# The second score product over 128 rows: the keys' low part as a tile per head

## The chip, the cores and the metric

One core of a Trainium2 chip runs the whole kernel in one launch. The metric is the time of one execution on the device in microseconds (us), as the median of several runs. A core has a tensor engine (PE, which multiplies a stationary tile, held in its array, with a moving one that streams through), VectorE (DVE), ScalarE (ACT), GpSimd (POOL), and SyncE (SP), whose queue issues almost all DMA transfers here. Each engine works through its own instructions in their order and waits for others by semaphores.

## The reference

Two layers of a decoder trunk on 512 tokens of 1024 features. Each layer has a SwiGLU feed-forward part (FFN), a token mixing and a second FFN, each behind an RMSNorm with a shift and scale from a condition vector. The mixing has 16 heads of 64 features in three groups:

```
scale = 64 ** -0.5
A (4 heads): softmax(q k' * scale, causal) v            # block-sparse; at 512 tokens every causal key is selected
B (4 heads): softmax over the 128 best causal keys of each query, ranked by an indexer:
             I[t, s] = sum_j w[t, j] * relu(q_idx[t, j] . k_idx[s])      # 8 indexer heads of 64
C (8 heads): stick-breaking: sigmoid(z) * prod over later keys of (1 - sigmoid(z)),  z = q k' * scale, s < t
o = headRMS(concat(A, B, C)) * out_g;   x = x + g2 * (o @ w_out)
```

q and k of groups A and B are normed per head and partly rotated; those of the indexer are rotated. All is float32.

## The kernel before, in words

Activations lie with features on partitions and tokens along the free axis. PE takes float32r operands; a float32 value v is carried as two of them, H = float32r(v) and L = float32r(v - H). A large product (`mm3`, lines 308 to 310) is three products added in PSUM: H.H, H.L and L.H. Weights come from HBM in pieces of 128 x 1024: SP loads a piece (`raw`, line 268, three buffers), ACT takes its H (`whi`, line 270), VectorE its L (`wlo`, line 280).

Scores contract over the 64 features of a head, half of the 128 partitions. The two heads of a pair lie on the two halves. To fill the rows, the kernel stacks parts. The q of head e is one tile whose own half (64 rows) holds H and whose other half holds L. The k of head e is one tile with H on both halves. One product over 128 rows then gives Hq.Hk + Lq.Hk. The missing Hq.Lk is a second product into the same PSUM area. It contracts over the 64 rows of the head's own half, and one tile holds the L of both heads' keys, each on its own half. So score products come in pairs, the first 128 rows deep, the second 64 rows deep (line 612).

The tiles are made so. ACT writes H of both heads (line 577) and VectorE L (line 578), each over 128 partitions. Then SP copies halves from partition to partition by DMA (`move`, line 603): three copies for a q pair, three for a k pair. All these tiles come from one pool of 12 buffers of 128 x 512, `qk`. A new tile waits until an older one is released by its last reader. The indexer's k is written with its two halves equal from the start and needs no copy.

The scores of a pair of heads come in three units. Unit 0 holds query tiles 0 and 1 of both heads: eight score products, four of 256 and four of 128 columns. Units 1 and 2 hold query tiles 2 and 3 of one head each. In group C they have keys on partitions and eight products (six of 256, two of 128 columns). In groups A and B they have queries on partitions and four products (two of 512, two of 384). The indexer has eight heads, each with four such products for query tiles 2 and 3, and for query tile 1 eight products of 256 columns for every four heads. Per layer this makes 208 score products. After the scores come the weights on ACT and VectorE, products with a triangular matrix (group C, line 705) or transpositions (A and B, line 769), then the outputs (line 656): eight products per unit over 128 rows.

The work of a layer's mixing is cut into steps, and a list, `PLAN`, names the order in which they are issued. The build's scheduler then moves instructions within it. Projections, which are long runs of `mm3`, stand between the steps of the attention, as does the top-k of group B, long runs of VectorE work (lines 853 and 854).

Of the kernel before, what the change touches and what calls it, by code (L numbers as in the profile page):

```python
"""Two layers of a conditioned hybrid decoder trunk on one core.

Activations are feature-major ([feature, token]) on chip, so that every weight is used in its own
layout as the stationary operand.  A float32 operand of a large product is carried as two float32r
parts, H = float32r(v) and L = float32r(v - H), and a product is H.H + H.L + L.H in float32 PSUM.

With 512 tokens and blocks of 256 there is at most one past block per query, and the block
top-k always selects it: group A attends to every causal key.  Group B's queries t < 128 have at
most 128 causal keys, all of which its top-128 holds; later tiles rank their keys on chip.
"""  # L10
# [16 lines left out]
P = 128  # L27
# [9 lines left out]
HD = 64  # L37
# [10 lines left out]
# Score tiles of a pair of heads come in three units, each two PSUM banks wide: query tiles 0 and 1  # L48
# of both heads (a bank each), then query tiles 2 and 3 of each head.  A block is (head, index, column in PSUM,
# column in SBUF, width).  # L50
#   with keys on partitions: index is the key chunk, and its columns are the unit's queries from
#   that chunk on; with queries on partitions: index is the query tile, and its columns its keys.
# [15 lines left out]
# Small constants: name, shape in a partition, needed by the first norm or later.  # L68
# [12 lines left out]
def head_chunks(l, f):  # L81
    """d_ff chunks that run side by side at the start of an FFN, while its input is still being made."""
    return list(range(4 if (l, f) == (0, 0) else 2))
# [41 lines left out]
# The order in which the steps of the mixing are issued.  A name that comes again is the next step of  # L125
# the same work: u = a unit of a pair's attention (scores and weights, their transposition or sums,
# outputs), n = norm of a pair's heads, c = q and k of a pair of group C, a and b = q and k of groups
# A and B, i = indexer scores, t = top-k of a query tile, v = values, h = split of a pair's output,
# o = output projection of group C.  w loads a weight piece ahead of its use.
# [53 lines left out]
class Net:  # L183
# [24 lines left out]
    def load(self, names, early):  # L208
        """One tile of small constants: a view per name."""
        shapes = [(n, s) for n, s, e in SMALL if e == early]  # L210
        t = self.cp.tile([P, sum(int(np.prod(s)) for _, s in shapes)], F32, name=names)
        self.nc.sync.dma_start(t, self.io[names])
        o, out = 0, []
        for _, s in shapes:
            w = int(np.prod(s))
            v = t[:, o:o + w]
            if len(s) > 1:
                names_ = "abc"[:len(s)]
                v = v.rearrange("p (%s) -> p %s" % (" ".join(names_), " ".join(names_)),
                                **{c: int(d) for c, d in zip(names_, s)})  # L220
            out.append(v)
            o += w
        return out

    def setup(self):
        """What the first norm needs."""
        nc = self.nc
        self.tc.keep_in_program_order(nc.scalar.preload_act_table_set("silu_and_others"))
        for m in range(0, KC, 2):
            nc.sync.dma_start(self.xs[:, m:m + 2, :], self.io["x"][:, m:m + 2, :])  # L230
        self.open_ada()
        self.first_w = [self.load_ada(0, 1, 0, 6)]
        self.normg, self.bada = self.load("early", True)
        self.first_w.append(self.load_ada(0, 0, 0, 6))
        self.ident = self.t(self.fp, "ident", [P, P])
        nc.sync.dma_start(self.ident, self.io["ident"])
        ones = self.cp.tile([P, 4], F32, name="ones")
        nc.gpsimd.memset(ones, 1.0)
        nc.gpsimd.memset(ones[HD:, 2:3], 0.0)
        nc.gpsimd.memset(ones[:HD, 3:4], 0.0)  # L240
        self.ones2, self.bones = ones[:, 0:2], ones[:, 2:4]
        self.mod = {}
# [19 lines left out]
    def fetch(self):  # L262
        """Loads a weight piece and takes its H."""
# [30 lines left out]
    def later(self, us, fn):  # L294
        """Has fn emitted once products of about us more microseconds have been."""
        self.delayed.append([us, fn])
# [16 lines left out]
    def rsqrt(self, ss, shape, inv, r=None, wide=None, pin=False):  # L313
        """With r: of ss * r * r * inv, and times r.  wide: where to write each, repeated."""
# [53 lines left out]
    def ada_first(self):  # L368
        """The shift and scale of the first norm, feature chunk by feature chunk."""
# [8 lines left out]
    def ada_all(self, items):  # L378
        """Modulation vectors, a half of one at a time."""
# [22 lines left out]
    def norm_rms(self, cs, pin=False):  # L402
        """1 / rms of the tokens of cs, a token tile per column."""
# [8 lines left out]
    def norm_wide(self, y, cs):  # L412
        """The same over all partitions."""
# [39 lines left out]
    def ffn_head(self, l, f, halves, prepare=lambda k: None):  # L453
        """First products of the FFN, chunk by chunk of its input."""
# [17 lines left out]
    def ffn(self, l, f, filler, head):  # L472
        """Generator: yields (m, tokens) for each finished part of the output."""
# [68 lines left out]
    def proj_tok(self, l, grp, tiles, evac):  # L542
        """Token-major projection, two steps per token tile: evac(t, psum)."""
# [27 lines left out]
    # Scores contract over 64 features: H.H and L.H go together, as a head's q with H on its own half  # L571
    # of the partitions and L on the other, and its k with H on both.
# [7 lines left out]
    def put_q(self, out, ps, scale=1.0, lo=0):  # L580
        """Features of a pair of heads, from token lo on, in two steps: adds a tile per head."""
# [9 lines left out]
    def put_k(self, out, ps, scale=1.0):  # L591
        """Adds a tile of H per head, and one of L, in two steps."""
        a, b, l = self.new_qk(3)
        self.split_feat(ps, scale, a, l)
        out.append((a, b, l))
        yield
        self.move(b[HD:], a[HD:])
        self.move(b[:HD], a[HD:])
        self.move(a[HD:], a[:HD])
        yield  # L600
# [4 lines left out]
    def scores(self, out, q, k, e, qs, ks, keys_out, start, stop):  # L605
        """Products of a head's q and k: of the columns qs and ks, with keys on partitions or queries."""
        own = slice(64 * e, 64 * e + 64)
        parts = [(q[e][:, qs], k[e][:, ks]), (q[e][own, qs], k[2][own, ks])]
# [6 lines left out]
    def do_rope(self, x, heads, tiles, table):  # L615
        """x: [P, len(tiles), heads, HD] view, rotated in place."""
# [12 lines left out]
    def to_feat(self, src, tiles, put):  # L629
        """src(t): token-major [P, 128] -> put(features by tokens), a step and those of put."""  # L630
# [6 lines left out]
    # Values of a pair of heads: token tile, head, H or L, feature.  A head's H and L are stationary  # L637
    # together, and their products with the weights are added when they leave PSUM.
# [3 lines left out]
    def put_v(self, v, t, ps):  # L642
        """ps: [P, 128] of one pair of heads."""
# [4 lines left out]
    def unit_out(self, pair, u, z, att):  # L648
        """Outputs of a unit, in its score tile, in two steps."""
# [18 lines left out]
    def finish_pair(self, l, pair, cs=slice(0, S)):  # L668
        """RMSNorm of both heads of a pair, in five steps."""
# [26 lines left out]
    def stick(self, pair, q, k, u):  # L696
        """Stick-breaking attention of a unit, keys on partitions, in seven steps."""
# [40 lines left out]
    def soft(self, pair, q, k, u, bias):  # L738
        """Softmax attention of a unit, queries on partitions, in seven steps.  The weights stay without
        their sums' division, which the norm of the heads makes up for.  # L740
        bias(t): [P, 128 * (t + 1)] added to the scores of query tile t."""
# [33 lines left out]
    def index_k(self, l):  # L775
# [30 lines left out]
        def put(ps):  # L806
# [3 lines left out]
            self.qk["ki"] = hi, hi, lo  # L810
# [15 lines left out]
    def index_heads(self, heads):  # L826
        """Adds four indexer heads to the scores, in ten steps."""
# [19 lines left out]
    def topk(self, t):  # L847
        """The top-128 keys of a query tile (lowest index first among equals) as an additive bias."""
# [11 lines left out]
    def gained_rope(self, l, gi):  # L860
        """The rotation's tables times a gain, and the gain of the other features on partitions."""
# [9 lines left out]
    def qk_ab(self, l, name, grp, gi):  # L871
        """Normed, rotated q and k of a pair of heads of group A or B, feature-major."""
# [46 lines left out]
    def finish_half(self, l, cs):  # L919
        """The last pair's norm and split for a token half."""  # L920
        yield from self.finish_pair(l, 3, cs)
        self.split_o(3, cs)
        yield

    def steps(self, l):
        """The mixing's work by name, each a generator of its steps."""
# [62 lines left out]
    def out_first(self, l, m):  # L989
        """Output projection of group C, in two steps."""  # L990
# [7 lines left out]
    def out_last(self, l):  # L998
        """Output projection of groups A and B, and the start of the next norm."""
# [20 lines left out]
    def ffn_norm(self, out, l, i):  # L1020
        """Adds up the next norm as the FFN's output comes."""
# [127 lines left out]
```

## Time and profile before

| | |
|---|---|
| median of 3 runs | 2210.2 us (2207.52 to 2212.14) |
| span of the profiled execution (first to last instruction) | 2206.9 us |
| mean granted PE clock | 0.991 |
| score products | 416, first at 431.4 us, last at 1794.2 us |

The profiled execution's own time is its span, 2206.9 us; the runs of the table were not profiled. In the profile each engine has busy times; PE's products are pipelined, so the times of single products overlap, and PEld is the loading of the stationary tile, which has an instruction of its own. A group row reads: line, engine, operation, output<-inputs, shape, number | busy us, mean ns of one | idle time before them and what ended it. `64*128` before the shape means 64 rows and 128 columns of the array. A row of stretches reads: stretch, its length, then busy us and instructions of each engine, the granted clock as a share of full speed, the DMA engines' busy share, and GB/s. A row of waits reads: who waited for whom, us in total, times, longest. A row of DMA issues ends with the us from issue to landing. The chain is the work that ended last, followed back from the end, without overlaps.

### The profile page before, as it was taken

The numbers are of one execution on the slowest core, as the hardware profiler recorded it, in microseconds if no ns is written. First come the engines' busy times: TensorE is split into PE (matmuls) and PEld (weight loads), VectorE is DVE, ScalarE is ACT, GpSimd is POOL, SyncE is SP. The second block draws the span as 40 slices with busy tenths as digits, with TensorE's granted clock in tenths as the row PEclk, the third lists the DMA queues.
The fourth block names the chain that finished last, engine by engine and source line by source line (L and its number), as shares of the span: only waits on it lengthen the run. The fifth ranks groups of instructions, "written<-read, shape, count | busy, mean of one in ns | idle before, by whom it ended". The sixth has DMA issues, their size and how long they took to land.

```text
span 2206.9 us, 28693 instructions
## 1 busy us (share of the span) xinstructions
PE 2171.1 (98%) x11280; PEld 1833.1 (83%) x11280; DVE 1308.5 (59%) x2607; ACT 832.6 (38%) x1295; POOL 3.5 (0%) x12
## 2 busy tenths in 40 slices
PE   6999999999999999999999999999999999999999
PEld 5888888878988988888898888887788888888888
DVE  8663744679979777375374333364799787333332
ACT  3422222456655432132242222234565644222220
POOL 0000000000000000000000000000000000000000
PEclk9999999999999999999999999998999999999999
DMA  7873842431222378385243333324222222333331
GB/s 292 272 267 97 288 140 82 111 80 50 76 70 80 120 249 283 99 267 191 86 132 115 96 96 97 96 73 115 58 71 65 75 72 87 96 96 96 97 98 63
DMA packets 82310, 275.45 MB, mean 125 GB/s; under 512 B 9984, under 2 KB 12544, under 8 KB 82176
## 3 DMA queue, kind: packets, MB, share of 16 engines
q1 hardware_dynamic: 80736, 271.53, 39.6%
q8 instruction: 88, 1.44, 0.3%
q10 hardware_dynamic: 1440, 2.10, 0.3%
q14 instruction: 46, 0.38, 0.1%
HBM read 256.55 MB, written 2.10 MB: 117 GB/s over the span
## 4 chain that ended last, share of the span: by engine, by line
PE 92%; DVE 5%; DMA 2%; ACT 1%; issue 1%; DVEq 0%; ACTq 0%
PE z L308 23%; PE z L310 23%; PE z L309 23%; PE z L612 6%; PE b L308 4%; PE b L310 4%; PE b L309 4%; PE z L656 2%; PE z L705 1%; DVE wlo L280 1%; DMA raw<-in_w_dram 1%; PE z L769 1%; DMA qk<-qk 1%; DVE att L568 1%; PE b L679 1%; PE b L633 1%
## 5 line engine op out<-in xcount | busy, mean ns | idle before, releaser
L280 DVE TENSOR_TENSOR wlo<-raw,whi 128x1024 fp32r<-128x1024 f32 (+1 forms) x338 | 412.2, 1220 | 542.1 <-ACT whi L270 540.1
L270 ACT CAST whi<-raw 128x1024 fp32r<-128x1024 f32 (+1 forms) x338 | 354.6, 1050 | 876.0 <-PE z L309 789.1
L308 PE MATMUL z<-hh,whi 128*128 128x512 f32 (+1 forms) x1616 | 597.2, 370 | 6.7 <-DVE xs L986 3.9
L309 PE MATMUL z<-hl,whi 128*128 128x512 f32 (+1 forms) x1616 | 597.2, 370 | 0.5
L310 PE MATMUL z<-hh,wlo 128*128 128x512 f32 (+1 forms) x1616 | 596.2, 369 | 1.3 <-DVE wlo L280 1.3
L308 PEld LDWEIGHTS z<-hh,whi 128*128 128x128 f32 x1616 | 306.0, 190 | 58.6 <-DVE xs L986 4.3
L310 PEld LDWEIGHTS z<-hh,wlo 128*128 128x128 f32 x1616 | 306.1, 190 | 52.7 <-DVE wlo L280 1.8
L309 PEld LDWEIGHTS z<-hl,whi 128*128 128x128 f32 x1616 | 306.4, 190 | 52.1 <-DVE hl L430 1.3
L308 PE MATMUL z<-gh,whi 128*128 128x512 f32 (+1 forms) x792 | 293.5, 371 | 0.0
L309 PE MATMUL z<-gl,whi 128*128 128x512 f32 (+1 forms) x792 | 292.8, 370 | 0.0
L310 PE MATMUL z<-gh,wlo 128*128 128x512 f32 (+1 forms) x792 | 289.1, 370 | 0.0
L349 DVE CUSTOM_DVE_ANT_0 adaw<-adaw,silc 128x1024 f32<-128x1024 f32 x144 | 170.9, 1221 | 30.1 <-DMA adaw<-in_w_ada_dram 30.1
L308 PEld LDWEIGHTS z<-gh,whi 128*128 128x128 f32 x792 | 149.0, 188 | 29.6
L310 PEld LDWEIGHTS z<-gh,wlo 128*128 128x128 f32 x792 | 149.1, 188 | 27.6
L309 PEld LDWEIGHTS z<-gl,whi 128*128 128x128 f32 x792 | 149.1, 188 | 26.5
L308 PE MATMUL b<-whi,hh 128*128 128x256 f32 x544 | 158.1, 291 | 0.0
L309 PE MATMUL b<-wlo,hh 128*128 128x256 f32 x544 | 156.1, 287 | 0.0
L310 PE MATMUL b<-whi,hl 128*128 128x256 f32 x544 | 156.0, 287 | 0.0
L612 PE MATMUL z<-qk,qk 64*128 64x256 f32 (+7 forms) x416 | 138.3, 392 | 1.5 <-DMA qk<-qk 1.5
L612 PEld LDWEIGHTS z<-qk,qk 128*128 128x128 f32 (+1 forms) x416 | 78.5, 189 | 56.9 <-issue 26.6
L506 DVE SCALAR_TENSOR_TENSOR xs<-z,mod,xs 128x512 f32<-128x512 f32 (+1 forms) x72 | 49.7, 691 | 124.5 <-PE z L310 124.4
L308 PEld LDWEIGHTS b<-whi,hh 128*128 128x128 f32 x544 | 105.7, 194 | 1.2 <-issue 0.6
(144 smaller groups left out, 2348.3 us busy)
## 6 DMA issues: line engine op xcount, KB each, us to landing
raw<-in_w_dram SPq DMA_DIRECT2D x332, 512.0 KB, 3.6
adaw<-in_w_ada_dram SPq DMA_DIRECT2D x144, 512.0 KB, 4.7
qk<-qk SPq DMA_DIRECT2D x96, 128.0 KB, 2.2
qk<-qk SPq DMA_DIRECT2D x24, 96.0 KB, 3.0
xs<-in_x_dram SPq DMA_DIRECT2D x4, 512.0 KB, 5.7
raw<-in_w_dram SPq DMA_DIRECT2D x4, 492.0 KB, 3.4
silc<-in_c_dram SPq DMA_DIRECT2D x3, 512.0 KB, 5.1
out_dram<-xs ACTq DMA_DIRECT2D x6, 256.0 KB, 2.0
```

The source lines that it names most:

```text
L270: nc.scalar.copy(hi[:, :n], raw[:, :n])
L280: self.nc.vector.tensor_sub(lo[:, :n], raw[:, :n], hi.bitcast(F32)[:, :n])
L308: mm(out, l[0], r[0], start=start, stop=False, **kw)
L309: mm(out, l[0], r[1], start=False, stop=False, **kw)
L310: mm(out, l[1], r[0], start=False, stop=stop, **kw)
L349: r = self.nc.vector.tensor_tensor_reduce(w, w, self.silc, 1.0, 0.0, op0=ALU.mult, op1=ALU.add, accum_out=m[:, j:j + 1])
L506: nc.vector.scalar_tensor_tensor(self.x[m][:, cs], ps[:, cs], gate[:, m:m + 1], self.x[m][:, cs], op0=ALU.mult, op1=ALU.add)
L568: nc.vector.tensor_sub(unit_sbuf(lo, u), src, unit_sbuf(hi.bitcast(F32), u))
L612: self.nc.tensor.matmul(out, a, b, start=start and i == 0, stop=stop and i == 1, skip_group_check=True)
L633: self.nc.tensor.transpose(ps[:, t * P:(t + 1) * P], src(t), self.ident)
L656: nc.tensor.matmul(outs[e][:, HT - w:], lhs, a[:, o:o + w], start=i + j == 0, stop=c == KEY_UNITS[u][-1][1] and j == 1, skip_group_check=True)
L679: nc.tensor.matmul(ss[:, i, :], sq[:, t * P:(t + 1) * P], self.bones, start=True, stop=True)
```

## The change

The L of the keys gets the same treatment as the H: one tile per head with L on both halves of the partitions. The second score product then takes the whole q tile and the whole L tile of its head, 128 rows. It adds Hq.Lk + Lq.Lk, so the sum now holds the product of the two low parts as well, which the kernel before left out.

```diff
     def put_k(self, out, ps, scale=1.0):
-        a, b, l = self.new_qk(3)
+        a, b, l, m = self.new_qk(4)
         self.split_feat(ps, scale, a, l)
-        out.append((a, b, l))
+        out.append((a, b, l, m))
         yield
-        self.move(b[HD:], a[HD:])
-        self.move(b[:HD], a[HD:])
-        self.move(a[HD:], a[:HD])
+        for own, other in ((a, b), (l, m)):
+            self.move(other[HD:], own[HD:])
+            self.move(other[:HD], own[HD:])
+            self.move(own[HD:], own[:HD])
         yield

     def scores(self, out, q, k, e, qs, ks, keys_out, start, stop):
-        own = slice(64 * e, 64 * e + 64)
-        parts = [(q[e][:, qs], k[e][:, ks]), (q[e][own, qs], k[2][own, ks])]
+        parts = [(q[e][:, qs], k[i + e][:, ks]) for i in (0, 2)]
         for i, (a, b) in enumerate(parts):
             if keys_out:
                 a, b = b, a
             self.nc.tensor.matmul(out, a, b, start=start and i == 0, stop=stop and i == 1,
                                   skip_group_check=True)
...
-            self.qk["ki"] = hi, hi, lo
+            self.qk["ki"] = hi, hi, lo, lo
```

A k pair takes four tiles from the pool of 12 and six copies; there are eight k pairs in a layer, so 48 copies more in all. Comments were removed too, which shifts line numbers by one or two.

The change also moves instructions. SP, in the mixing of layer 0, at q and k of the second pair of group B (the last in the layer); `qk_1000` to `qk_1002` are its q tiles before, `qk_1025` and `qk_1026` its H tiles of k. Before:

```order
L268 DMA raw_1104_6451<-in_w_dram 128x1024
L603 DMA qk_1001_5953<-qk_1000_5952 64x512
L603 DMA qk_1001_5953<-qk_1002_5954 64x512
L603 DMA qk_1000_5952<-qk_1002_5954 64x512
L268 DMA raw_1107_6457<-in_w_dram 128x1024
L603 DMA qk_1026_6067<-qk_1025_6066 64x512 x2
L603 DMA qk_1025_6066<-qk_1025_6066 64x512
L268 DMA raw_1110_6463<-in_w_dram 128x1024
```

And now, with `qk_1007` to `qk_1009` for q, `qk_1032` and `qk_1033` for H of k, `qk_1034` and `qk_1035` for its L:

```order
L268 DMA raw_1112_6483<-in_w_dram 128x1024
L605 DMA qk_1008_5981<-qk_1007_5980 64x512
L605 DMA qk_1008_5981<-qk_1009_5982 64x512
L605 DMA qk_1007_5980<-qk_1009_5982 64x512
L268 DMA raw_1115_6489<-in_w_dram 128x1024
L605 DMA qk_1033_6095<-qk_1032_6094 64x512 x2
L605 DMA qk_1035_6097<-qk_1034_6096 64x512 x2
L605 DMA qk_1032_6094<-qk_1032_6094 64x512
L268 DMA raw_1118_6495<-in_w_dram 128x1024
L605 DMA qk_1034_6096<-qk_1034_6096 64x512
L268 DMA raw_1133_6632<-in_w_dram 128x1024
```

The copies of L go between those of H, and a weight load that followed the third copy now has three more copies around it.

PE, where that pair's unit 0 takes its scores, before:

```order
L690 MATMUL b_1038_6133<-rmat_513,of_965_5785 128x128 x3
L612 MATMUL z_1028_6078<-qk_1025_6066,qk_1000_5952 128x256
L612 MATMUL z_1028_6078<-qk_1027_6068,qk_1000_5952 128x256
L612 MATMUL z_1028_6078<-qk_1026_6067,qk_1001_5953 128x256
L612 MATMUL z_1028_6078<-qk_1027_6068,qk_1001_5953 128x256
L612 MATMUL z_1028_6078<-qk_1025_6066,qk_1000_5952 128x128
```

And now:

```order
L613 MATMUL z_1036_6110<-qk_1032_6094,qk_1007_5980 128x256
L770 MATMUL z_1041_6140<-rmat_513,tf_1023_6029 128x128 x7
L691 MATMUL b_1046_6165<-rmat_513,of_972_5813 128x128
L308 MATMUL b_1069_6270<-hh_970_5809,whi_1015_6006 128x512
L309 MATMUL b_1069_6270<-hl_971_5810,whi_1015_6006 128x512
L613 MATMUL z_1054_6206<-qk_1033_6095,qk_1008_5981 128x512
L613 MATMUL z_1054_6206<-qk_1035_6097,qk_1008_5981 128x512
L613 MATMUL z_1054_6206<-qk_1033_6095,qk_1008_5981 128x384
L613 MATMUL z_1054_6206<-qk_1035_6097,qk_1008_5981 128x384
L613 MATMUL z_1036_6110<-qk_1034_6096,qk_1007_5980 128x256
L613 MATMUL z_1036_6110<-qk_1033_6095,qk_1008_5981 128x256
L613 MATMUL z_1036_6110<-qk_1035_6097,qk_1008_5981 128x256
```

The second product reads `qk_1034` for head 0 and `qk_1035` for head 1, where before both read `qk_1027`. The scheduler put other work of PE between the first product and the first that needs the L tiles. Over the whole program the order on PE differs only in such places, and the splits of q and k on ACT stand where they stood.

## The prediction

> **What bounds the kernel now.** I read the page's busy shares first, then the chain that ended last, then the waits of PE in the mixing of layer 0, then which lines fill that chain.
>
> ```profile
> span 2206.9 us, 28693 instructions
> PE 2171.1 (98%) x11280; PEld 1833.1 (83%) x11280; DVE 1308.5 (59%) x2607; ACT 832.6 (38%) x1295; POOL 3.5 (0%) x12
> ...
> PE 92%; DVE 5%; DMA 2%; ACT 1%; issue 1%; DVEq 0%; ACTq 0%
> PE z L308 23%; PE z L310 23%; PE z L309 23%; PE z L612 6%; PE b L308 4%; PE b L310 4%; PE b L309 4%; PE z L656 2%; PE z L705 1%; DVE wlo L280 1%; DMA raw<-in_w_dram 1%; PE z L769 1%; DMA qk<-qk 1%; DVE att L568 1%; PE b L679 1%; PE b L633 1%
> ```
>
> The tensor engine (PE) is busy for 98% of the span and makes 92% of the chain. The score products, L612, are 6% of the chain: some 132 us, and all of it lies in the two mixings, nowhere in the FFNs. The longest wait of PE between 420 and 860 us is this one:
>
> ```profile
> PE z L308 <- DVE xs L986: 1.9, 1, 1.9
> ```
>
> So in the mixing PE hardly waits for anybody, and what makes its own instructions shorter is worth something until another engine falls behind. The question is how long a score product takes, and who is next.
>
> **What a score product costs.** Two rows of the groups by shape, and the row of all of them:
>
> ```profile
> L612 PE MATMUL z<-qk,qk 64*128 64x256 f32 (+7 forms) x416 | 138.3, 392 | 1.5 <-DMA qk<-qk 1.5
> ...
> L612 PE MATMUL z<-qk,qk 64*128 64x384 f32 x32 | 14.6, 455 | 0.0
> L612 PE MATMUL z<-qk,qk 128*128 128x384 f32 x32 | 14.5, 452 | 0.0
> ```
>
> These durations overlap one another, so they do not show the price. Starts do. From the timeline of PE:
>
> ```profile
> 433.23 0.28 PE L308 MATMUL b<-whi,hh 128*128 128x256 f32 x1
> 433.35 1.22 PE L612 MATMUL z<-qk,qk 128*128 128x256 f32 x4
> 434.49 0.39 PE L309 MATMUL b<-wlo,hh 128*128 128x256 f32 x1
> ...
> 469.69 0.39 PE L308 MATMUL b<-hh,whi 128*128 128x512 f32 x1
> 469.92 3.16 PE L612 MATMUL z<-qk,qk 128*128 128x512 f32 x8
> ```
>
> An ordinary product of 256 columns is followed by the next start after 0.12 us (433.23 to 433.35), one of 512 after 0.23 us (469.69 to 469.92). In both places the product that follows is the first of a score group, a 128-row one, and it starts on time. But four score products of 256 columns take 1.14 us (433.35 to 434.49), 0.285 each. They alternate between 128 and 64 rows, so each one stands beside a product of another row count. The chain of waits gives the same for each kind of group (start, us on the chain):
>
> ```profile
> 433.51 1.05 PE z L612 x4
> ...
> 470.08 3.00 PE z L612 x8
> ...
> 502.79 0.23 PE b L310
> ...
> 503.71 2.07 PE z L612 x8
> ...
> 573.09 2.19 PE z L612 x8
> ...
> 614.98 0.90 PE z L656 x8
> ```
>
> The outputs of a unit, L656, are the twin of its scores: eight products, the same column counts, a new stationary tile each, always 128 rows. They take 0.90 us, the scores 2.07 (unit 0) or 2.19 (units 1 and 2 of group C). I read the difference as a price of every change of the row count, about 0.16 us, which the change removes by making all scores 128 rows deep.
>
> One rule of the Trainium skill speaks against this reading: the page "TensorE: Matmul & The Clock Gate", Part 3, The mechanism, says that a weight load overlaps running matmuls only when it goes to another row group. By it, making both kinds 128 rows deep would gain nothing. This trace contradicts it: products of 128 rows, each with its own load, start 0.12 us apart. The page "TensorEngine Tiling (Array Packing)", Key Properties, says that changing the tiling mode drains the array; that fits, but no run here shows a drain as such. No number below needs either page.
>
> **The change, part by part.**
>
> *Score products.* Per layer, at the chain's prices: 8 units of index 0: 2.07 - 0.90 = 1.17 each, 9.4 us. 8 units 1 and 2 of group C: 2.19 - 0.90 = 1.29, 10.3 us. 16 groups of 512+512+384+384 columns (8 softmax units, 8 indexer heads): 3.00 / 2 = 1.50 now; at 0.23 and, between 0.12 and 0.23, 0.175 for 384 columns, 0.81 after; 0.69 each, 11.0 us. Two indexer units of eight 256-column products: 2 x 1.05 = 2.10 now, 0.96 after, 2.3 us in all. Together 33 us a layer, 66 in both. From the other side, the whole 138.3 us busy against 192 x 0.12 + 64 x 0.23 + 64 x 0.175 + 96 x 0.09 = 58 us leaves 80; 0.09 for 128 columns is the rest of L656's 0.90 after six of 0.12. I take 72, which is 0.52 of L612's busy time, of which the larger bound counts overlapping ends.
>
> *Clock.* Around the densest score groups the granted clock drops:
>
> ```profile
> 1518.00:1548.00 30.00, 28.89 (x110) 0.77 0.31 84
> ```
>
> 0.23 x 30 = 6.9 us are lost there alone. If the gate follows how dense the array's work is, part of it comes back. From nothing to 7 us; I take 4, since a good half of it lies on L612 itself and is in the 72 already.
>
> *What VectorE leaves.* This decides how much of the 72 is kept. Stretches of the two mixings, all engines (PE, PEld, DVE, ACT, POOL), then L612 alone in the same stretches:
>
> ```profile
> 420.00:480.00 60.00, 59.02 (x273) 42.80 (x273) 32.96 (x57) 29.02 (x40) 0.00 (x0) 0.97 0.36 93
> 480.00:620.00 140.00, 139.58 (x896) 123.16 (x895) 129.19 (x329) 89.30 (x144) 0.00 (x0) 0.99 0.26 69
> 620.00:740.00 120.00, 119.79 (x825) 105.98 (x825) 96.36 (x300) 65.03 (x151) 0.00 (x0) 1.00 0.27 83
> 1509.00:1569.00 60.00, 58.26 (x240) 41.53 (x239) 28.84 (x48) 24.86 (x35) 0.00 (x0) 0.89 0.34 87
> 1569.00:1709.00 140.00, 139.53 (x873) 121.91 (x874) 127.88 (x318) 87.70 (x135) 0.00 (x0) 0.98 0.25 66
> 1709.00:1829.00 120.00, 119.74 (x829) 106.40 (x829) 95.25 (x306) 65.67 (x155) 0.00 (x0) 1.00 0.24 68
> ```
>
> ```profile
> 420.00:480.00 60.00, 24.96 (x72) 13.41 (x72) 0.97 0.36 93
> 480.00:620.00 140.00, 25.01 (x84) 15.53 (x84) 0.99 0.26 69
> 620.00:740.00 120.00, 18.01 (x52) 9.63 (x52) 1.00 0.27 83
> 1509.00:1569.00 60.00, 24.67 (x67) 13.22 (x67) 0.89 0.34 87
> 1569.00:1709.00 140.00, 27.74 (x90) 17.04 (x90) 0.98 0.25 66
> 1709.00:1829.00 120.00, 17.96 (x52) 9.62 (x52) 1.00 0.24 68
> ```
>
> First stretch (indexer scores, first pair of C): PE saves 0.52 x 24.96 = 13.0 us and VectorE is busy for 33 of 60, so all of it counts; 12.8 in layer 1. Second stretch: PE could save 13.0 (14.4), but VectorE already works 129.2 (127.9) of 140, so no more than 10.8 (12.1) can be had, and its handing over to ACT and back is in those gaps. I take 4.5 in each layer, between 0 and 11. Third stretch: 9.4 (9.3) on PE against 96 of 120 on VectorE; I take 8. Sum 25.5 + 25.3 = 51.
>
> *More copies.* Each of the 16 key tiles now needs six SBUF copies instead of three: 48 more.
>
> ```profile
> qk<-qk SPq DMA_DIRECT2D x96, 128.0 KB, 2.2
> ...
> L603 SPq DMA_DIRECT2D qk<-qk x120: 461/462/785, 421.3 to 1781.9; - x120
> ...
> 681.34 5.51 SPq L603 DMA_DIRECT2D qk<-qk  x3
> ...
> 689.33 2.32 PE L612 MATMUL z<-qk,qk 128*128 128x256 f32 x8
> ```
>
> The third copy of a tile overwrites what the first two read, so it waits for a landing (2.2 us). The two chains run one inside the other: the new one adds three issues of 0.46 us, 1.4 us, to SP for each key, and at most 1.4 + 2.2 = 3.6 us if its landing is paid apart. Behind them in SP's queue stand weight loads. Mostly the scores come 10 us and more after the copies. At the last pair of group B they do not: the three copies end at 686.85, the last lands 2.2 us later, about 689.0, and the scores start at 689.33. There 1.4 us is late; likewise the weight loads behind it. I charge 3 us in all, between 0 and 16 x 3.6 = 58.
>
> *Tiles and instructions on ACT and VectorE.* The fourth tile of a key is written by copies alone: ACT and VectorE get no instruction more, and the products' count stays 416.
>
> Sum: 51 + 4 - 3 = 52 us. The profiled execution's span is 2206.9 us, 3.3 below the median of 2210.2, so I take the difference off the median: 2158 us.
>
> **Rivals.** *VectorE lets PE have it all*: its order carries the slack of the thin stretches over. For it: it is idle for 41% of the span. Against: its 92% in the second stretch. 66 to 87 us less: 2123 to 2144, say 2134. *VectorE takes nearly all*: behind the first stretch the chains PE, ACT, VectorE, PE get no shorter. For it: PE and VectorE are both over 90% there. Only the first stretches count, 26 us less 3: 2187. *The row count is not what costs*: L612 is slow for a reason that both forms share, such as its weight load in the same rows. For it: 452 against 455 ns above. Against: the first product of each group starts on time, and L656. Then nothing is gained and 3 us are lost: 2213, within the noise. *The pool of 12 tiles runs dry, slower than before*: a key now holds four tiles to the end of its pair's scores instead of three, so copies wait for older scores, and weight loads wait behind them on SP.
>
> ```profile
> SPq L603 <- PE z L612: 8.4, 2, 4.2
> ```
>
> This has happened twice, at 4.2 us each. If it comes with every key and each also pays the 3.6 us, a key costs 7.8 us; ten of the 16 reaching PE undo the 72, fourteen cost 109 and give 2210 + 37 = 2247. Against it: in the order of the changed kernel the splits of q and k on ACT stand where they stood, and PE has other products between.
>
> **How the numbers follow.** The forecast, 2158 (own range 2144 to 2175), has 0.62; all to PE 0.14; VectorE takes nearly all 0.14; no gain 0.05; pool dry 0.05. Differences under 0.2%, 4.4 us, count as none. The first three are faster: 0.90; same 0.05, slower 0.05. The range holds the forecast, most of the full gain and the nearer half of the third: 2128 to 2188.
>
> **What would show it.** Right: no 64-row form of the score line; a softmax unit's four scores at about 0.8 us on the chain and a unit's eight at 0.9; L612's share of the chain from 6% to under 3%; new waits of PE for VectorE or ACT in the second stretch and VectorE's share there above 95%; the granted clock in the first stretch of layer 1 above 0.89. Wrong: eight scores still near 2 us (then the row count was not the cause), or PE waiting for copies or weights by more than some us a layer.

## The result, and the profile after

| | before | changed kernel |
|---|---|---|
| median, first comparison | 2211.17 us (2207.52 to 2212.47) | 2145.63 us (2145.13 to 2149.47) |
| ratio, 95% interval | | 0.9714 (0.9700 to 0.9727) |
| median, a second comparison | 2206.94 us | 2146.83 us, 0.9720 (0.9702 to 0.9737) |
| span of the profiled execution | 2206.9 us | 2147.7 us |
| mean granted PE clock | 0.991 | 0.996 |

The changed kernel is 60 to 66 us faster, 2.8 to 2.9%. 52 us were forecast. The page of its profile, the parts that answer to those shown of before:

```profile
span 2147.7 us, 28762 instructions
PE 2094.9 (98%) x11280; PEld 1806.0 (84%) x11280; DVE 1305.2 (61%) x2607; ACT 831.2 (39%) x1295; POOL 2.9 (0%) x12
...
PE 82%; DVE 12%; ACT 2%; DMA 2%; issue 1%; SPq 0%; ACTq 0%; DVEq 0%
PE z L308 23%; PE z L310 23%; PE z L309 23%; PE b L308 3%; PE b L310 3%; PE b L309 3%; DVE att L568 2%; DVE sc L855 2%; DVE wlo L280 2%; DVE m L854 1%; PE z L613 1%; DMA qk<-qk 1%; PE z L657 1%; PE z L706 1%; DVE tf L718 1%
```

The score products, now line 613, went from 6% of the chain to 1%. VectorE went from 5% to 12%: chain pieces in the mixing now run through its top-k and its splits. The chain of the changed kernel (start, us on the chain):

```profile
532.66 0.90 PE z L613 x8
...
608.98 0.88 PE z L657 x8
...
616.40 0.81 PE z L613 x4
...
626.44 0.88 PE z L613 x8
```

Eight scores now take what eight outputs (L657) take, 0.88 to 0.90 us instead of 2.07 to 2.19. Four scores of a softmax unit take 0.81 instead of 1.50. No 64-row form of the line is left. The timeline says the same of four products of 256 columns, which took 1.14 us:

```profile
433.30 0.64 PE L613 MATMUL z<-qk,qk 128*128 128x256 f32 x4
433.77 0.28 PE L309 MATMUL b<-wlo,hh 128*128 128x256 f32 x1
```

That is 0.47 us from start to start, 0.12 each. Added up over all 416 from the trace's records, the time from the start of a score product to the start of PE's next product fell from 134.2 us to 68.5. At 0.12, 0.23, 0.175 and 0.09 us for the four widths it would be 58.

Stretches of the mixings in the changed kernel (columns as before). They lie near the work of the earlier ones, but do not hold the same: the second of layer 0 has 806 of PE's products, not 896.

```profile
420.00:470.00 50.00, 46.59 (x274) 40.61 (x274) 30.84 (x54) 27.23 (x38) 0.00 (x0) 0.97 0.46 118
470.00:590.00 120.00, 115.53 (x806) 106.71 (x805) 118.01 (x295) 83.33 (x129) 0.00 (x0) 0.99 0.32 85
590.00:707.00 117.00, 114.18 (x846) 106.90 (x845) 99.67 (x312) 66.50 (x158) 0.00 (x0) 1.00 0.36 102
1484.00:1530.00 46.00, 42.99 (x259) 37.19 (x258) 30.09 (x52) 25.36 (x36) 0.00 (x0) 1.00 0.45 119
1530.00:1660.00 130.00, 125.51 (x888) 116.67 (x887) 127.88 (x324) 89.35 (x140) 0.00 (x0) 0.99 0.33 87
```

In the second stretch VectorE is at 98% of the time (118.0 of 120, 127.9 of 130), and PE, at 99.7% before, at 96%. How long the same work takes is read from the starts of the products that have the same number in PE's order (about 2% of the products stand elsewhere in that order, so this holds to about 1 us). Lengths in us:

| stretch before | before | changed, first and second profile | saved | forecast |
|---|---|---|---|---|
| 420 to 480 | 60 | 49.9, 48.0 | 10 to 12 | 13.0 |
| 480 to 620 | 140 | 130.8, 130.0 | 9 to 10 | 4.5 |
| 620 to 740 | 120 | 114.9, 115.0 | 5 | 8 |
| 1509 to 1569 | 60 | 43.9, 43.0 | 16 to 17 | 12.8 |
| 1569 to 1709 | 140 | 128.4, 127.6 | 12 | 4.5 |
| 1709 to 1829 | 120 | 114.5, 114.4 | 5 to 6 | 8 |

PE now waits where it hardly waited before (1.5 us for the copies, 0.2 for `att`, nothing listed for `v`):

```profile
PE z L613 <- DMA qk<-qk: 5.5, 5, 1.9
PE z L657 <- DVE att L568: 4.7, 8, 1.1
...
PE b L308 <- DVE v L647: 3.6, 2, 1.8
```

How long a mixing takes is read from products of the norms, L408. Each norm has two groups of them, one for each half of the tokens; a mixing is counted from the second group of the norm ahead of it to the first group of the norm behind it. Before, both layers, then the changed kernel:

```profile
390.65 0.58 PE L408 MATMUL b<-ones,nacc 128*128 128x2 f32 x4
...
730.87 0.51 PE L408 MATMUL b<-ones,nacc 128*128 128x2 f32 x4
...
1479.50 0.58 PE L408 MATMUL b<-ones,nacc 128*128 128x2 f32 x4
...
1826.44 0.51 PE L408 MATMUL b<-ones,nacc 128*128 128x2 f32 x4
```

```profile
391.14 0.58 PE L408 MATMUL b<-ones,nacc 128*128 128x2 f32 x4
...
707.02 0.51 PE L408 MATMUL b<-ones,nacc 128*128 128x2 f32 x4
...
1455.17 0.58 PE L408 MATMUL b<-ones,nacc 128*128 128x2 f32 x4
...
1767.59 0.51 PE L408 MATMUL b<-ones,nacc 128*128 128x2 f32 x4
```

Layer 0 went from 340.2 us to 315.9, layer 1 from 346.9 to 312.4. All of the gain, 58.8 of 59.2 us, lies in the two mixings. From one profile to the next the length of one layer's mixing moves by some 3 us, so the sum of both counts more than their difference.

### The profile page after: what moved, and what is told of

Read it like the earlier page. It is cut to its first block, busy times and chain, and to the rows that moved or that the text cites. A ratio compares the mean times of both kernels' runs of the same rounds, so it can differ in the third digit from the quotient of the medians.

```text
span 2147.7 us, 28762 instructions
## 1 busy us (share of the span) xinstructions
PE 2094.9 (98%) x11280; PEld 1806.0 (84%) x11280; DVE 1305.2 (61%) x2607; ACT 831.2 (39%) x1295; POOL 2.9 (0%) x12
## 4 chain that ended last, share of the span: by engine, by line
PE 82%; DVE 12%; ACT 2%; DMA 2%; issue 1%; SPq 0%; ACTq 0%; DVEq 0%
PE z L308 23%; PE z L310 23%; PE z L309 23%; PE b L308 3%; PE b L310 3%; PE b L309 3%; DVE att L568 2%; DVE sc L855 2%; DVE wlo L280 2%; DVE m L854 1%; PE z L613 1%; DMA qk<-qk 1%; PE z L657 1%; PE z L706 1%; DVE tf L718 1%
## 5 line engine op out<-in xcount | busy, mean ns | idle before, releaser
L309 PEld LDWEIGHTS b<-wlo,hh 128*128 128x128 f32 x544 | 105.7, 194 | 0.2
L310 PEld LDWEIGHTS b<-whi,hl 128*128 128x128 f32 x544 | 105.6, 194 | 0.0
## 6 DMA issues: line engine op xcount, KB each, us to landing
qk<-qk SPq DMA_DIRECT2D x144, 128.0 KB, 2.3
```

What stands on the lines that cost most here:

```text
L309: mm(out, l[0], r[1], start=False, stop=False, **kw)
L310: mm(out, l[1], r[0], start=False, stop=stop, **kw)
```

## The experiments

In the table, the mixings are read as above, and the scores are the time from each score product's start to PE's next start, added up.

| kernel | median us | ratio (95%) | mixing of layer 0, 1 | scores |
|---|---|---|---|---|
| before | 2207 to 2211 | 1 | 340, 347 | 134.2 |
| changed | 2145.6, 2146.8 | 0.9714, 0.9720 | 316, 312; again 313, 312 | 68.5, 67.5 |
| 128 rows, no copies | 2138.4, 2140.8 | 0.9678 (0.9663 to 0.9693), 0.9691 (0.9673 to 0.9709) | 308, 311; again 309, 312 | 63.3, 62.7 |
| copies alone | 2212.6 | 1.0006 (0.9989 to 1.0022) | 344, 344 | 136.4 |
| products grouped | 2153.7 | 0.9743 (0.9726 to 0.9760) | 315, 315 | 76.2 |
| changed, half the top-k | 2143.2 | 0.9697 (0.9681 to 0.9713) | 310, 310 | 64.7 |
| before, half the top-k | 2210.8 | 0.9998 (0.9985 to 1.0011) | 344, 343 | 134.3 |
| copies from GpSimd | 2163.7 | 0.9794 (0.9774 to 0.9814) | 322, 318 | 74.3 |
| 128 rows, pool of 10 | 2143.2 | 0.9703 (0.9685 to 0.9721) | 310, 311 | 66.1 |
| 128 rows, one product | 2125.9 | 0.9618 (0.9594 to 0.9641) | 302, 301 | 35.7 |
| the same, half the top-k | 2115.8 | 0.9579 (0.9561 to 0.9598) | 298, 296 | 34.2 |

### The rows without the copies

```diff
-        own = slice(64 * e, 64 * e + 64)
-        parts = [(q[e][:, qs], k[e][:, ks]), (q[e][own, qs], k[2][own, ks])]
+        parts = [(q[e][:, qs], k[e][:, ks]), (q[e][:, qs], k[2][:, ks])]
```

This is the kernel before with one line changed: three tiles and three copies for a key, but the second product runs over all rows of both.

> The second product is 128 rows deep, but the keys keep three tiles and three copies: both heads' L stay on one tile, so the stack adds the q low part of one head times the k low part of the other head, a term of two low parts that the reference does not have. Theory (the price is the change of row count, the copies only cost): all of the gain comes without the copies, 2137 to 2146 us, that is the change's 2145.6 or up to 8 us less. Rival (the fourth tile and its copies help, through the order that the build makes): 2155 or more. Rival (the row count is not the cause): about 2211.

2138.4 us: the row count alone gives all of the gain, and 7.2 us more than the change as a whole. By the traces PE's products stand in the same order as before, product for product, so on PE nothing but the rows differs. Measured again beside the changed kernel:

> The kernel with 128 rows and no copies more, measured again beside the changed kernel: it keeps the term of one head's low part of q times the other head's low part of k. Theory (the copies cost the changed kernel some 7 us): 2136 to 2141 us, at least 4 less than the changed kernel of the same comparison. Rival (the 7 us were the chip and the moment): within 3 us of it.

> The changed kernel itself, for the comparison on the same chip: 2143 to 2149 us by both theories. By the theory that the row count also sets the granted clock, its windows at half clock add up to 20 us or less again, against 41 in the profile of the kernel before.

2140.8 against 2146.8 us, 6.0 less, so the difference is real. About 5 us of it stand behind the score products (63 against 68 us). The waits of PE for copies differ less, 4.0 us in the second profile of this kernel against 3.9 in the second of the changed one, 3.5 against 5.5 in the first ones, so they do not explain it alone. The changed kernel differs in one thing more: the scheduler put about 2% of PE's products elsewhere. The windows at half clock, counted from the clock's records, were 10 us in the second profile of the changed kernel and 17 in the first, against 41 before.

### The copies without the rows

```diff
-        parts = [(q[e][:, qs], k[i + e][:, ks]) for i in (0, 2)]
+        own = slice(64 * e, 64 * e + 64)
+        parts = [(q[e][:, qs], k[e][:, ks]), (q[e][own, qs], k[2 + e][own, ks])]
```

> The fourth tile and all six copies per key as in the change, but the second product reads 64 rows of them, as before. Theory: no gain and a small price of the copies, 2211 to 2219 us. Rival (the gain comes from the tiles or the order, not from the rows): 2160 or less.

1.0006, not to be told from no change. The same 48 copies and 16 tiles that go with 6 to 7 us in the changed kernel cost nothing measurable, at most 5 us by the interval, while PE takes 134 to 136 us for the scores. Together with the kernel before this one, whose order is the old one, this rules out that tiles or order make the gain. That the price of the copies depends on how fast PE comes for their results is likely, but not shown: PE's order is not quite that of the changed kernel here either.

### All 128-row products first, then all 64-row products

```diff
-        for i, (a, b) in enumerate(parts):
-            ...
+        for i in range(2):
+            for out, q, k, e, qs, ks, keys_out, start, stop in jobs:
+                own = slice(64 * e, 64 * e + 64)
+                a, b = [(q[e][:, qs], k[e][:, ks]), (q[e][own, qs], k[2][own, ks])][i]
...
```

The three places that call `scores` hand it all products of a group at once; they are not shown.

> The kernel before, but each group takes all its 128-row products first and then all its 64-row products, so the row count changes 136 times instead of 416; tiles and copies as before. Theory (each change costs 0.18 us): PE saves 280 x 0.18 = 51 us, of which 60 to 85% arrive: 2168 to 2181 us. Rival (a 64-row product costs more by itself, wherever it stands): no gain, 2205 to 2215. Rival (64-row products of the two halves run side by side once they are neighbours): below 2160.

2153.7 us: the same products as before, 208 of them still 64 rows deep, are 57 us faster only because of their order. So it is not the 64 rows that cost but going from one row count to the other. It also beats the theory's own number, and the last rival is right about a part. Timeline and chain of this kernel:

```profile
431.96 0.50 PE L612 MATMUL z<-qk,qk 64*128 64x256 f32 x4
...
432.39 0.39 PE L308 MATMUL b<-whi,hh 128*128 128x256 f32 x1
```

```profile
459.39 1.00 PE z L612 x4
...
464.61 1.02 PE z L612 x8
```

The first is a unit of the indexer, whose heads alternate between the two halves of the partitions. Four 64-row products of 256 columns and the way back to 128 rows take 0.43 us, less than the 0.48 of four 128-row ones: in the records, two of different halves start 3 ns apart. That is the side-by-side running, which helps unit 0 and the indexer's query tile 1. In the other groups all 64-row products are of the same half. The chain's 1.00 and 1.02 us leave out a part of the groups' ends. From the first start to PE's next product behind the group, four take 1.10 us (1.49 alternating, 0.81 with 128 rows), eight take 1.11 (2.28, 0.89). So a visit to 64 rows, in and out, costs 0.2 to 0.3 us a group. It does not grow with the number of products: of four in a row (256, 256, 256 and 128 columns) the next start comes after 0.222, 0.119, 0.116 and 0.147 us, so the second and third run like 128-row ones.

The estimate of 51 us for PE was not far from the 134.2 - 76.2 = 58 measured. That only 60 to 85% would arrive was wrong, since 57 arrived; but these are not simply the 58. In the mixings PE's other products took 11 us more, most of it waits. The time at half clock fell from 41 to 7 us, which by the same estimate as below under Clock gave about as much back.

### Less work for VectorE

```diff
         for i in range(TOPK // 8):
-            m8 = self.t(self.sp, "m8", [P, 8], bufs=2)
-            nc.vector.max(m8, sc)
-            nc.vector.match_replace(sc, m8, sc, TAKEN)
+            if i % 2:
+                m8 = self.t(self.sp, "m8", [P, 8], bufs=2)
+                nc.vector.max(m8, sc)
+                nc.vector.match_replace(sc, m8, sc, TAKEN)
```

> The changed kernel with every other round of the top-k left out (64 keys found instead of 128), some 28 us less of VectorE work in each layer. Theory (VectorE holds back a part of the gain in the second stretch): 2128 to 2139 us, 6 to 17 less than the change. Rival (PE still sets the pace there, VectorE costs nothing): 2143 to 2148.

> The kernel before with every other round of the top-k left out, some 28 us less of VectorE work in each layer, as it was left out of the changed kernel. Theory (PE sets the pace in both): 2204 to 2211 us, not over 5 less than before. Rival (VectorE held the kernel before back too, so the forecast's stretches misread it): 2195 or less.

VectorE's busy time fell by 22 us a layer (1305.2 to 1260.8 us in both), not 28. In the kernel before it is worth nothing (0.9998), as PE's waits in the mixing of layer 0 said, 1.0 us between 420 and 740. In the changed kernel it is worth 2.4 to 3.6 us by the medians, 4 to 5 by the ratios to the kernel before, and the intervals overlap. That is less than the theory's least, 6; 2143.2 us lies in the rival's range. The stretch from 480 to 620 us of the changed kernel, whole top-k and half:

```profile
480.00:620.00 140.00, 135.57 (x998) 128.35 (x998) 136.56 (x365) 95.03 (x166) 0.00 (x0) 0.99 0.32 87
```

```profile
480.00:620.00 140.00, 136.76 (x1026) 129.93 (x1025) 114.12 (x291) 96.60 (x171) 0.00 (x0) 1.00 0.33 89
```

VectorE falls from 136.6 to 114.1 of 140 us, and PE gets 28 products more into the stretch, 2.8%. VectorE at 97% was close to being the bound, but held PE back little: the work of the two second stretches of the table above takes 128.0 and 125.6 us, 2 to 3 less each.

### How much further PE's savings arrive

```diff
-        parts = [(q[e][:, qs], k[e][:, ks]), (q[e][:, qs], k[2][:, ks])]
+        parts = [(q[e][:, qs], k[e][:, ks])]
...
```

The one product left then also ends the sum; that line is not shown.

> The kernel with 128 rows and no copies more, without the second score product at all (H and L of q times H of k only, so the scores lose the keys' low part): 208 products of 128 rows less, 29 us of PE at 0.12 us for 256 columns, in the same stretches in which the change saved. Theory (PE sets the pace of the mixing still, VectorE holds nothing back): 2108 to 2120 us, some 20 to 29 less than with them. Rival (VectorE at 97% of the second stretch is the bound now): 2130 to 2140.

> The kernel with one score product only (no low part of the keys), and with every other round of the top-k left out too. Theory (VectorE took the half of the 29 us that did not arrive): 2108 to 2117 us, 9 to 18 less than with the whole top-k. Rival (it went to waits on single results, copies, weights and hand-overs, which less VectorE work does not shorten): 2121 to 2127.

2125.9 us, between theory and rival. The score lines fell by 27 us, and 12 to 16 arrived. With half the top-k left out as well it is 2115.8, 9 to 10 less; in the changed kernel the same cut gave 2 to 5. The stretch from 470 to 590 us, whole top-k and half:

```profile
470.00:590.00 120.00, 115.33 (x832) 107.37 (x831) 118.10 (x310) 85.48 (x144) 0.00 (x0) 1.00 0.27 76
```

```profile
470.00:590.00 120.00, 117.61 (x851) 109.69 (x849) 106.13 (x267) 85.81 (x147) 0.00 (x0) 1.00 0.30 80
```

So VectorE does hold PE back, as the forecast had it, but mainly one step later: of what the change takes from PE most arrives, of the next 27 us only a half, and most of the other half comes back with less work for VectorE.

### What the copies cost by

```diff
-        for own, other in ((a, b), (l, m)):
-            self.move(other[HD:], own[HD:])
-            self.move(other[:HD], own[HD:])
-            self.move(own[HD:], own[:HD])
+        for own, other, eng in ((a, b, self.nc.sync), (l, m, self.nc.gpsimd)):
+            for out, src in ((other[HD:], own[HD:]), (other[:HD], own[HD:]), (own[HD:], own[:HD])):
+                eng.dma_start(out.bitcast(F32), src.bitcast(F32))
```

> The changed kernel with the three new copies of a key issued from GpSimd's queue instead of SP's. Theory (the copies cost by standing ahead of weight loads and of H's third copy in SP's queue): most of the 7 us comes back, 2138 to 2142. Rival (they cost by the L tiles being late, or by the fourth tile in the pool): 2144 to 2152.

2163.7 us, far outside both: taking the copies out of SP's queue made it 17 us slower than the changed kernel. DMA issues and the first row of PE's waits:

```profile
qk<-qk SPq DMA_DIRECT2D x96, 128.0 KB, 2.2
qk<-qk POOLq DMA_DIRECT2D x48, 128.0 KB, 3.6
```

```profile
PE z L612 <- DMA qk<-qk: 19.0, 11, 3.8
```

A copy issued from GpSimd lands after 3.6 us, not 2.2, and PE waits for copies for 19.0 us instead of 3.9 to 5.5. The time at half clock rose with it, to 27 us from 10 and 17. The run shows that a late L tile costs PE directly. It does not show what the copies' place in SP's queue is worth, since it moved both.

The pool, with the kernel of 128 rows without copies:

```diff
-        return [self.t(self.mp, "qk", [P, S], F32R, bufs=12) for _ in range(n)]
+        return [self.t(self.mp, "qk", [P, S], F32R, bufs=10) for _ in range(n)]
```

> The kernel with 128 rows and no copies more, with 10 buffers in the pool instead of 12: two q tiles and three k tiles of a pair press on 10 about as two and four do on 12. Theory (the fourth tile costs by the pool): 2142 to 2150 us. Rival (the pool has room, the copies themselves cost): 2136 to 2141.

2143.2 against 2140.8 us: 2.4 more, in the theory's range, but the ranges of the runs (2141.3 to 2144.2, 2138.1 to 2141.9) overlap a little. A tighter pool can be a part of the 6 us. How they divide between late L tiles, SP's queue, the pool and PE's other order stays open.

## Why the prediction was right

**What bounds the kernel.** That PE sets the pace of the mixing before and hardly waits for anybody was right: half the top-k is worth nothing there.

**The price of a row count change.** Right, and shown from both sides: the rows alone give 66 to 72 us, the order alone 57. The forecast had 72 us on PE, between 66 and 80; with the widths' own cadence, 134.2 - 58 = 76 was there to be had. The changed kernel's score lines fell by 65.7 and 66.7, in part because PE now waits at some of them. The mechanism, a price per change, is right as far as it goes, but it is not one constant. It is 76 / 416 = 0.18 us when every product changes, while the first change of a group can cost as little as 0.09 (0.21 us to the next start, not 0.12), and a whole visit, two changes, 0.2 to 0.3.

**The rule that spoke against.** A weight load that overlaps only with other rows (the Trainium skill, "TensorE: Matmul & The Clock Gate", Part 3, The mechanism) would have left no gain. The runs contradict it for 128 rows after 128 rows, 0.12 us apart. The forecast passed over that the same section of the Trainium skill also has PE pull a load ahead when it goes to the background weight buffer. Read so, it does not speak against the gain; no run here shows where a load goes. Another statement of the Trainium skill, same page, Part 3, Measured speedup vs the span model, is that each further tile packed beside another adds about 4 ns; the grouped kernel agrees, with 3 ns between the starts.

**What VectorE leaves.** This is the term that was mis-sized. The forecast let VectorE take 21 us away (72 to 51), most in the second stretches, where it left 4.5 of 13 to 14. They gave 9 to 12, nearly all of the 10.8 and 12.1 that VectorE's gaps allowed. The step that failed is "its handing over to ACT and back is in those gaps". VectorE did rise to 98% there, and its listed waits fell from 9.2 us (480 to 620, before) to 0.7 (470 to 590, changed): the gaps were mostly slack. A likely reason is that ACT, which VectorE waited for, itself waited for PE, 18.3 us for L705 in that stretch before; no run isolates it. What VectorE now costs is smaller than 21 by both measures: PE's idle time that the records put down to it rose from 6.5 to 16.8 us in both mixings together, and taking 22 us a layer of top-k away gives 2 to 5 us back.

**Clock.** 4 us were taken beyond the scores, "since a good half of it lies on L612 itself". The mean clock rose from 0.991 to 0.996 and 0.998: (1 - 0.991) x 2206.9 = 20 us lost before, 5 to 9 after, 12 to 15 less. By the clock's records, 8 of the 41 us at half clock lay on score products before, 2 and 0 after. Products of 512 columns start 0.427 us apart in such windows and 0.227 outside, so half the time of a window is lost, as an estimate: 3 to 4 us of the gain lie on the scores and 9 to 11 beside them. A fifth lay on L612, not a good half. The records also tell two kinds of windows apart. In the three kernels that alternate, four or five windows start after PE has been shown as busy for all of the 3.4 us before (at 447, 498, 1539 and 1590 us in the kernel before); they last 20 to 24 us together. In the ten profiles of the others there is none of these: PE was idle for about a quarter or more of the 3.4 us ahead of each window.

**Copies.** 3 us were charged; 6 to 7 is measured, copies, tiles and order together, within 0 to 58. In the kernel before, the copies' price was too small to measure. At the last pair of group B, the one place where the forecast expected them late, by 1.4 us, PE waits 0.4 to 0.9 us for them.

**Rivals.** "VectorE lets PE have it all" gave 2123 to 2144, and 2138 to 2141 is reached without the copies: about VectorE it was nearer than the forecast, and the change lies between the two. "VectorE takes nearly all" fails by the second stretches. "The row count is not what costs" is refuted by the grouped kernel. "The pool runs dry" cost at most a few us.

**The sum.** Added up from the records of both mixings, first and second profile of the changed kernel, the clock's part as an estimate: PE's score lines fell by 66 and 67 us (72 forecast), the clock beside them gave 7 and 10 there (4 forecast), and PE's other products took 14 and 15 us more, mostly waits (24 forecast, for VectorE and copies). That is 59 and 62 for 52. That the first two errors nearly cancel is luck; what is left of the miss is the waits, VectorE's above all.

## What to carry to other kernels

Look at starts, not at durations: 455 and 452 ns for the two forms hid that each of them cost 0.18 us too much, and the twin with the same column counts (the outputs) gave the price at once. Do not alternate products of different row counts: make them the same, or where that costs copies, put those of one kind together; order alone was worth 57 us here. Before copying data to fill the rows, see whether what lies there already is harmless: with the other head's low part in those rows, the added term is a product of two low parts, and the kernel is 6 to 7 us faster than the change, at 2138.4 us.

## What the runs showed of the hardware

- Alternating between 128 and 64 rows: start to start 0.31 us at 256 columns, either way, where 128 rows after 128 rows take 0.12.
- 64-row products of different halves, once they stand together, start 3 ns apart: four of 256 columns and the way back in 0.43 us. Of the same half they start 0.12 us apart from the second on, like 128-row ones.
- The granted clock goes with it: in the profiles, alternating kernels 0.990 to 0.991 (38 to 44 us at half clock), the others 0.994 to 0.999 (3 to 27 us), though PE is shown as busy for 97 to 98% in all of them. The 0.994 is the kernel with the late copies.
- An SBUF copy of 128 KB lands 2.2 us after its issue on SP's queue and 3.6 us after one on GpSimd's, and each one keeps GpSimd itself busy for 0.52 us.
